# Counting the length classes with a matmul, and a new order of the first batch's preparation, in a ragged self-attention kernel

## The chip, the cores and the metric

One core of one Trainium2 chip runs the kernel. The metric is the device time of one execution in microseconds. The engines of the core are TensorE (PE; PEld is its weight load), VectorE (DVE), ScalarE (ACT), GpSimd (POOL) and SyncE (SP, which here issues most transfers). They run side by side, each with its own instruction stream, and wait for one another by semaphores.

## The reference

There are 32 sequences with up to 512 rows of 512 values, and a length for each, drawn from 64 to 511. For each sequence, only its first `seq_len` rows count, with 8 heads of 64:

```
qkv = x[b, :seq_len] @ w_qkv                      # 512 -> 3 * 512
scores = (q @ k.T) / sqrt(64)                     # per head
attn = exp(scores - max); attn = attn / (sum(attn) + 1e-08)
output[b, :seq_len] = (attn @ v) of all heads     # the rest of the rows is zero
```

## The kernel before, in words

The kernel sorts the 32 sequences by length, longest first, and works them off in pairs. Each pair belongs to a **class**: the number of rows that its longer sequence is rounded up to. `CLASSES` holds 16 values, 512, 480, 448 and so on down to 64 in steps of 32, and 340 between them. Every engine has one loop body for each class, and the index of a pair's class, read from the tile `cls`, says which body is next. Within a body, the attention of one sequence (scores, exponentials, product with v, division) is interleaved with the projections (q, k, v) of the next one.

The order on each engine is written out by hand: a `Prog` holds a list of operations for PE, ACT and DVE, and what is added first is issued first. `acquire` (L283) makes PE wait until a PSUM bank has been emptied, `evacuate` (L301) lets DVE or ACT empty it. An engine never overtakes in its own list. Everything the change touches lies in the first 25 us, before the loops.

**Sorting** (the DVE block at the end, from L1872, and the PE block). DVE makes a key of each length, finds the largest (`top`, from which SP learns the address of the longest sequence and issues the loads of its four tiles of 128 rows, `load_tiles` L1474), and ranks the keys into `onehot`. Two small matmuls (L1860) put the sorted lengths and the sorted indices into PSUM bank `pav`; DVE copies the indices to `idx` and the lengths to `n_s`. Each step goes through a `Chain` (L124), which waits for its last instruction before it issues the next one. The constants of this part (`pos_f`, `rk_f`, `sel` and others) are iotas on POOL, and the last of them raises `s_iota`, on which DVE's first step waits; the thresholds `thr_f` are three of these iotas, one row of 16 pairs by 15 classes. Then POOL makes the identity for the transposes.

**Zero matmuls.** `warm(e, n)` (L961) issues n matmuls of zeros, 512 columns each. There are nine at the start, eight behind the sorting matmuls, and six behind the first two transposes.

**The first batch** (`make_prologue`, L965). The four tiles of x land one after another. DVE casts each to half precision (`cast_x`, L1021), PE transposes it in four pieces (`transposes`, L969), and DVE or ACT copies the result to `xT` (`copy`, L981: tiles 1 and 3 on DVE, 0 and 2 on ACT). ACT meanwhile casts the weights as they land (`cast_w`, `cast_v`). The projections of the first two pairs of heads are done in halves of 256 columns, so that tiles 0 and 1 suffice to begin: `first_half(0)` to `first_half(3)`, each four matmuls, into banks a0, a1, v0 and v1, then `second_half(0)` to `second_half(3)`, each followed by DVE's cast of the whole bank to `qkT` (L1014).

PE's order is: transposes of tiles 0 and 1, six zero matmuls, transposes of tile 2; then, once banks a0 and a1 are free (copies 0 and 1) and the weights are there, first halves 0 and 1, transposes of tile 3, first halves 2 and 3; then, after copies 2 and 3, the second halves. DVE's order is: `first_masks`, casts of tiles 0, 1 and 2, copy 1, cast of tile 3, copy 3, `class_table`, then the casts of the four banks.

**The masks and the classes.** `first_masks` (L1160) clamps the lengths to at least 1 (`n_k`) and compares the row numbers with the first length, once for the keys and once for the queries; the result is needed when DVE empties the first v projection and when POOL writes a column of ones. `class_table` (L1139) compares each pair's length with the 15 thresholds, sums, converts to integers and raises `s_cls`, on which `begin_loops` (L1189) of each engine waits.

**The rest of the prologue** is a list of steps (the loop over tokens "Q2 K2 S0 S1 Q3 K3 V0 S2 S3 V1 X2 V2 X3 V3" in `make_prologue`). Q and K are projections of the next pairs of heads (DVE empties them, L423), S are scores of the first pair (ACT takes the exponential), V are projections of v (DVE empties them with the mask), X are transposes of the second batch. Banks a0 and a1 take turns, so a step waits until the bank of the step before the last has been emptied: Q2 waits for the cast of `second_half(0)`, Q3 for that of Q2, V0 for that of Q3. POOL fills some tiles (L1787), casts the second batch's first two tiles when they land (L1796) and writes the ones.

Of the kernel before, what the change touches and what calls it, by code (L numbers as in the profile page):

```python
# [7 lines left out]
FP32 = mybir.dt.float32  # L8
F16 = mybir.dt.float16
I32 = mybir.dt.int32  # L10
AF = mybir.ActivationFunctionType
ALU = mybir.AluOpType

P = 128
# [3 lines left out]
NR = 40  # L18
EARLY = 2
STEP = 32  # L20
# [10 lines left out]
DENSE_ROWS = 340  # L31
CLASSES = sorted([STEP * k for k in range(2, 17)] + [DENSE_ROWS], reverse=True)
# [120 lines left out]
def kernel(  # L153
# [17 lines left out]
    def sb(name, shape, dt):  # L171
        return nc.alloc_sbuf_tensor(name, shape, dt).ap()

    def sem(name):
        return tc.alloc_semaphore(name)
# [23 lines left out]
    pos_f = sb("pos_f", [B, B], FP32)  # L199
    pos_c = sb("pos_c", [B, 1], FP32)  # L200
    rk_f = sb("rk_f", [B, NR], FP32)
    thr_f = sb("thr_f", [1, B // 2, len(CLASSES) - 1], FP32)
    ident_f = sb("ident_f", [P, P], FP32)
    ident = sb("ident", [P, P], F16)
    cls_f = sb("cls_f", [1, B // 2], FP32)
    cls = sb("cls", [1, B // 2 + 2], I32)
    idx = sb("idx", [1, NR], I32)
    steps = sb("steps", [1, B, 4], I32)
# [25 lines left out]
    s_iota = sem("s_iota")  # L234
    s_hot = sem("s_hot")
    s_srt = sem("s_srt")
    s_id = sem("s_id")
    s_cross = sem("s_cross")
    s_cls = sem("s_cls")
# [721 lines left out]
    def warm(e, n):  # L961
        for _ in range(n):
            e.matmul(psc[:, 1, 0, :], zt16[:, 0:P], zt16[:, 0:MAXS], start=True, stop=True)

    def make_prologue():  # L965
# [6 lines left out]
        def transposes(t):  # L972
            def tr(e):
                e.wait_ge(s_c0[t], 1)
                for c in range(NC):
                    ins = e.transpose(
                        home[t][:, c * P : (c + 1) * P], x16[0][:, t, c * P : (c + 1) * P], ident
                    )
                ins.then_inc(s_t0[t], 1)

            pr.add("pe", tr)  # L981

        def copy(t, g):
            src = home[t][:, 0:D].rearrange("p (c n) -> p c n", n=P)
            dst = xT[0][:, :, t * P : (t + 1) * P]
            pr.take(g, s_t0[t])
            fn = lambda e: (e.copy if g == "act" else e.tensor_copy)(out=dst, in_=src)
            pr.add(g, lambda e: fn(e).then_inc(free[copied[t]], 1))
            pr.busy[copied[t]] = True
# [8 lines left out]
        def first_half(k):  # L998
            mms = list(part(k, 0))
            pr.add("pe", lambda e: [fn(e) for fn in mms])  # L1000
# [20 lines left out]
        def cast_x(t):  # L1021
            def fn(e):
                e.wait_ge(s_x0[t], 16)
                e.tensor_copy(out=x16[0][:, t, :], in_=x_nat[0][:, t, :]).then_inc(s_c0[t], 1)

            pr.add("dve", fn)
# [12 lines left out]
        pr.add("pe", lambda e: e.wait_ge(s_id, 1))  # L1039
        for t in range(2):  # L1040
            transposes(t)
        pr.add("pe", lambda e: warm(e, 6))
        transposes(2)
        pr.add("dve", first_masks)
        cast_x(0)
        cast_x(1)
        cast_x(2)
        copy(1, "dve")
        cast_x(3)
        copy(3, "dve")  # L1050
        pr.add("dve", class_table)
        for c in range(NC):
            cast_w(0, c, last=c == NC - 1)
        copy(0, "act")
# [5 lines left out]
        pr.add("pe", lambda e: e.wait_ge(s_wr["qk"], 1))  # L1060
        first_half(0)
        first_half(1)
        transposes(3)
        first_half(2)
        first_half(3)
        acquire(pr, "s0")
        acquire(pr, "x0")
# [41 lines left out]
        for tok in "Q2 K2 S0 S1 Q3 K3 V0 S2 S3 V1 X2 V2 X3 V3".split():  # L1109
            f, i = tok[0], int(tok[1])  # L1110
            if f == "S":
                scores(pr, i % 2, 0, 0, i, 4, MAXS)
                continue
            if f == "X":
                second_batch(i, ("act", "dve")[i % 2])
                continue
            if f == "V":
                if i == 0:
                    pr.add("pe", lambda e: e.wait_ge(s_wr["v"], 1))
                if i == 3:  # L1120
                    pr.signals += [free[b] for b in halves_av]
                vproj(pr, bank, 0, i, 4)
            else:
                if i == 2:
                    pr.add("pe", lambda e, n=2 + "QK".index(f): e.wait_ge(s_wr["qk"], n))
                qk(pr, f"a{bank}", 0, [(i, "QK".index(f))], MAXS, MAXS)
            if tok == "Q2":
                pr.add("act", cast_v)
            elif tok == "Q3":
                pr.add("pe", lambda e: begin_loops(e))  # L1130
                cast_second(2)
            elif tok == "K3":
                cast_second(3)
            bank ^= 1
        pr.add("dve", mask_table)
        pr.take("pe", s_on[0])
        return pr

    def class_table(e):  # L1139
        q = Chain(e, s_self)  # L1140
        q.tensor_tensor(
            out=thr_f,
            in0=n_s[0:1, 0:B:2].unsqueeze(2).broadcast_to([1, B // 2, len(CLASSES) - 1]),
            in1=thr_f, op=ALU.is_le,
        )
        q.reduce_sum(out=cls_f, in_=thr_f, axis=mybir.AxisListType.X)
        q.tensor_copy(out=cls[:, 0 : B // 2], in_=cls_f)
        q.memset(cls[:, B // 2 : B // 2 + 2], len(CLASSES))
        q.signal(s_cls)

    def mask(q, o, n):
        k = n.shape[1]
# [34 lines left out]
        e.reg_load(k, cls[0:1, bass.ds(e.snap(r, min_val=0, max_val=B // 2 + 1), 1)])  # L1187

    def begin_loops(e):  # L1189
        e.wait_ge(s_cls, 1)  # L1190
        r, k = e.alloc_register("pair"), e.alloc_register("cls")
        e.reg_mov(r, 0)
        e.reg_load(k, cls[0:1, 0:1])
        regs[e.engine] = (r, k)
        if e.engine == nc.tensor.engine:
            regs["next"] = e.alloc_register("next")
            e.reg_add(r, r, 1)
            e.reg_load(regs["next"], cls[0:1, 1:2])
# [209 lines left out]
    with nc.Block() as block:  # L1408
# [335 lines left out]
        def _(e):  # L1744
# [9 lines left out]
            iota(rk_f[:, B:NR], [[0, NR - B]], B - 1, 0)  # L1754
            iota(sel[:, 1, :], [[0, P]], 0, 1)
            iota(row_f, [[P, NT]], 0, 1)
            at = CLASSES.index(DENSE_ROWS)
            for a, b in ((1, at), (at, at + 1), (at + 1, len(CLASSES))):
                iota(thr_f[:, :, a - 1 : b - 1], [[0, B // 2], [-STEP, b - a]], CLASSES[a], 0,
                     b == len(CLASSES))  # L1760
            q = Chain(e, s_pself)
            q.memset(ident_f, 0.0)
            q.affine_select(
                out=ident_f, in_=ident_f, compare_op=ALU.not_equal, fill=1.0,
# [31 lines left out]
                e.tensor_copy(out=x16[1][:, t, :], in_=x_nat[1][:, t, :]).then_inc(s_xc[1], 1)  # L1796
            e.wait_ge(s_tab, 1)
            ones(0, NT, masks[:, B, :, :])
            e.wait_ge(s_cls, 1)
            e.tensor_copy(out=steps[:, :, 0], in_=idx[:, 5 : B + 5]).then_inc(s_steps, 1)  # L1800
            e.tensor_copy(
                out=steps[:, :, 1].rearrange("o (p two) -> o p two", two=2),
# [51 lines left out]
        @block.tensor  # L1854
        def _(e):
            e.wait_ge(s_zero, 1)
            warm(e, 9)
            e.wait_ge(s_hot, 1)
            for k in range(2):
                ins = e.matmul(  # L1860
                    pav[:, k * NR : (k + 1) * NR], sel[:, k, :], onehot,
                    start=True, stop=True,
                )
            ins.then_inc(full[("av", "dve")], 1)
            warm(e, 8)
            regs["far"] = e.alloc_register("far")
            prologue.run("pe", e)
            e.wait_ge(s_ini, 7)
            graph(e, "pe", None, lambda e: bridge.run("pe", e))

        @block.vector
        def _(e):  # L1872
            q = Chain(e, s_self)
            e.memset(zt, 0.0).then_inc(s_zero, 1)
            e.wait_ge(s_iota, 1)
            e.wait_ge(s_len, 16)
            e.scalar_tensor_tensor(
                out=key_r, in0=len_b.rearrange("p (b two) -> p b two", two=2)[:, :, 0],
                scalar=float(B), in1=pos_f, op0=ALU.mult, op1=ALU.add,
            ).then_inc(s_self, 1)  # L1880
            e.wait_ge(s_self, 1)
            e.nop().then_inc(s_self, -1)
            q.max(out=top_f, in_=key_r[0:1, :])
            q.tensor_copy(out=top, in_=top_f)
            q.signal(s_top)
            e.wait_ge(s_lenc, 16)
            q.tensor_copy(out=sel[:, 0, :], in_=len_c[:, 0:1].broadcast_to([B, P]))
            q.tensor_scalar(out=key_c, in0=len_c[:, 0:1], scalar1=float(B),
                            scalar2=pos_c, op0=ALU.mult, op1=ALU.add)
            q.tensor_scalar(out=cmp, in0=key_r, scalar1=key_c, scalar2=0.0,  # L1890
                            op0=ALU.is_gt, op1=ALU.add, accum_out=rank)
            q.tensor_scalar(out=onehot, in0=rk_f, scalar1=rank, scalar2=None,
                            op0=ALU.is_equal)
            q.signal(s_hot)
            e.wait_ge(full[("av", "dve")], 1)
            e.nop().then_inc(full[("av", "dve")], -1)
            q.tensor_copy(out=idx, in_=pav[0:1, NR : 2 * NR])
            q.signal(s_srt)
            q.tensor_copy(out=n_s, in_=pav[:, 0:NR])
            q.join()  # L1900
            rank_reg[0] = e.alloc_register("rank")
            e.reg_mov(rank_reg[0], 0)
            now[0] = masks[:, B, :, :]
            prologue.run("dve", e)
            begin_loops(e)
            graph(e, "dve")
# [35 lines left out]
```

## Time and profile before

| what | value |
|---|---|
| median of three runs | 335.57 us (334.88 to 336.11) |
| profiled execution | 335.28 us |
| its span, first to last instruction | 333.5 us |
| mean granted clock of PE | 0.994 |
| busy: PE, ACT, DVE, POOL | 319.4, 246.4, 204.3, 67.5 us |
| casts of tiles 0 to 3 start (DVE) | 8.17, 8.64, 10.05, 10.92 us |
| Q2 starts (PE) | 15.46 us |
| first exponential starts (ACT) | 17.71 us |

The profile is of one execution; its times count from the first instruction. The span leaves out what lies around it, here 1.8 us. A row of the timeline gives the start, the time from there to the end of the group, engine, line, operation, the tile written and those read, the shapes, the count, and in brackets how long the engine was idle before and what ended it. Waits that the sequencer of an engine ends are marked with a q (DVEq L134 is a hand-over within a `Chain`).

### The profile page before, as it was taken

Reading aid. Unit: us, or ns where it says so; the run is one execution under the profiler, and the core shown is the slowest. Engines: PE = TensorE matmul, PEld = TensorE weight load, DVE = VectorE, ACT = ScalarE, POOL = GpSimd, SP = SyncE. Lnnn points to the kernel's source line nnn. Section 1 sums busy time; section 2 is a strip of 40 time slices with the busy share of each in tenths; the row PEclk is TensorE's granted clock in tenths of the full one; section 3 lists DMA queues with packets and bytes.
Section 4 is the critical chain, followed back from the end, with each engine's and each line's share of the span. In section 5 each row is a group of like instructions: output and inputs, shape, how many; then the busy total and the mean of one; then the engine's idle time right before and its main releaser. Section 6 shows DMA issues by size and latency. Waiting matters only on the chain. (4 is left out here: it accounts for less than half of the span.)

```text
span 333.5 us, 12290 instructions
## 1 busy us (share of the span) xinstructions
PE 319.4 (96%) x4345; PEld 206.8 (62%) x4346; DVE 204.3 (61%) x578; ACT 246.4 (74%) x359; POOL 67.5 (20%) x126
## 2 busy tenths in 40 slices
PE   6899999999999999999999999999999999999990
PEld 2665545455655656656566667677777777777760
DVE  3676576546484575576566567655755566666761
ACT  4568888788979879778878887887677676766540
POOL 3634020201101211210220222022111132131331
PEclk9999999999999999999999999999999999999997
DMA  6966699766555986985886798999689767788742
GB/s 196 355 185 223 200 395 239 273 153 216 141 206 128 336 254 161 303 291 161 264 304 174 226 303 202 263 260 231 196 148 205 198 183 165 161 199 159 205 140 71
DMA packets 83249, 72.34 MB, mean 217 GB/s; under 512 B 41628, under 2 KB 64156, under 8 KB 83172
## 3 DMA queue, kind: packets, MB, share of 16 engines
q1 hardware_dynamic: 71300, 59.84, 65.9%
q10 hardware_dynamic: 11872, 11.54, 10.1%
q8 instruction: 40, 0.66, 0.9%
q14 instruction: 37, 0.30, 0.3%
HBM read 25.32 MB, written 36.70 MB: 186 GB/s over the span
## 5 line engine op out<-in xcount | busy, mean ns | idle before, releaser
L350 ACT ACTIVATE ep<-psc 128x704 f16<-128x704 f32 (+8 forms) x196 | 156.7, 848 | 43.4 <-PE psc L307 32.4
L307 PE MATMUL pa<-xT,w_r 128*128 128x224 f16 (+19 forms) x952 | 121.7, 278 | 2.0 <-DVE qkT L1014 0.7
L307 PEld LDWEIGHTS pa<-xT,w_r 128*128 128x128 f16 (+1 forms) x952 | 70.8, 97 | 29.8 <-issue 9.2
L307 PE MATMUL psc<-qkT 64*128 64x352 f16 (+17 forms) x692 | 68.0, 288 | 0.7 <-PEq L61 0.2
L423 DVE CAST qkT<-pa 128x512 f16<-128x512 f32 (+9 forms) x60 | 34.5, 577 | 44.7 <-PE pa L307 40.4
L307 PE MATMUL pa<-w_r,xT 128*128 128x512 f16 (+4 forms) x332 | 57.9, 330 | 0.0
L307 PE MATMUL pav<-v_aug,ep 128*128 128x65 f16 x1254 | 55.0, 194 | 1.2 <-PEq L61 1.2
L307 PEld LDWEIGHTS pav<-v_aug,ep 128*128 128x128 f16 x1254 | 49.0, 98 | 9.9 <-issue 2.5
L307 PE MATMUL pav<-xT,w_r 64*128 64x352 f16 (+12 forms) x392 | 50.8, 307 | 0.0
L391 ACT ACTIVATE ep<-psc 128x960 f16<-128x960 f32 (+3 forms) x48 | 42.9, 953 | 9.1 <-PE psc L307 6.0
L422 ACT CAST qkT<-pa 128x320 f16<-128x320 f32 (+8 forms) x73 | 34.1, 471 | 18.3 <-PE pa L307 14.0
L1780 POOL MEMSET v_aug<- 128x256 f16 x24 | 7.5, 313 | 186.1 <-POOLq L1368 186.1
L644 DVE SCALAR_TENSOR_TENSOR onat<-pav,masks,rcp 128x128 f32<-128x128 f32 (+1 forms) x120 | 41.4, 384 | 4.2 <-DVE rcp L621 1.6
L307 PEld LDWEIGHTS psc<-qkT 64*128 64x128 f16 x692 | 26.4, 94 | 27.8 <-issue 17.2
L1774 POOL CAST x<-x_nat 128x1536 f16<-128x1536 f32 (+3 forms) x33 | 42.0, 1272 | 7.8 <-POOLq L1368 7.6
L446 DVE TENSOR_TENSOR v_aug<-pa,masks 128x512 f16<-128x512 f32 (+1 forms) x46 | 30.7, 673 | 16.7 <-PE pa L307 16.4
L307 PEld LDWEIGHTS pav<-xT,w_r 64*128 64x128 f16 (+1 forms) x392 | 26.6, 94 | 12.3 <-issue 1.3
L307 PEld LDWEIGHTS pa<-w_r,xT 128*128 128x128 f16 (+2 forms) x332 | 22.7, 98 | 16.6 <-issue 4.1
L307 PE MATMUL pav<-w_r,xT 128*128 128x512 f16 (+3 forms) x124 | 26.9, 350 | 0.0
L307 PEld LDWEIGHTS pa<-v_aug,ep 128*128 128x128 f16 x538 | 19.6, 98 | 7.2 <-issue 3.0
L621 DVE RECIPROCAL rcp<-pav 128x8 f32<-128x8 f32 (+2 forms) x65 | 12.7, 196 | 17.5 <-PE pav L307 14.5
L307 PE MATMUL pa<-v_aug,ep 128*128 128x65 f16 x538 | 22.3, 194 | 0.0
(86 smaller groups left out, 172.3 us busy)
## 6 DMA issues: line engine op xcount, KB each, us to landing
out_dram<-zt SPq DMA_DIRECT2D x16, 768.0 KB, 5.6
x_nat<-in_x_dram SPq DMA_DIRECT2D x12, 512.0 KB
x_nat<-in_x_dram SPq DMA_DIRECT2D x5, 1024.0 KB
out_dram<-onat ACTq DMA_DIRECT2D x12, 384.0 KB, 5.4
out_dram<-onat SPq DMA_DIRECT2D x12, 384.0 KB, 4.7
x_nat<-in_x_dram SPq DMA_DIRECT2D x17, 256.0 KB, 5.6
out_dram<-onat ACTq DMA_DIRECT2D x15, 256.0 KB, 3.6
x_nat<-in_x_dram SPq DMA_DIRECT2D x4, 768.0 KB
```

Source lines behind the costliest of these rows:

```text
L307: return lambda e: e.matmul(o, lhsT, rhs, start=start, stop=stop)
L350: return e.activation(out=dst[at], in_=src[at], func=AF.Exp, scale=scale)
L391: lambda e, par=par, b=b: e.activation(out=ep[:, i, par, 0:T, 0:N], in_=psc_f[:, par, 0 : T * N].rearrange("p (t n) -> p t n", n=N), func= ...
L422: return lambda e: e.copy(out=dst, in_=src)
L423: return lambda e: e.tensor_copy(out=dst, in_=src)
L446: return lambda e: e.tensor_tensor(out=v_aug[h][:, t, lo // HD : lo // HD + n, 0:HD], in0=area[b][:, 0:w].rearrange("p (a d) -> p a d", d=HD),
L621: pr.add("dve", lambda e: e.reciprocal(out=rv, in_=den).then_inc(s_r, 1))
L644: ins = e.scalar_tensor_tensor(scalar=now[0][:, 1, t : t + 1], op0=ALU.mult, op1=ALU.mult, **ops)
L1774: e.tensor_copy(out=x16[h][:, 0:T, :], in_=x_nat[h][:, 0:T, :]).then_inc(s_xc[h], 1)
L1780: e.memset(v_aug[h][:, T - 1, NPAIR:NH, 0:HD], 0.0)
```

## The change

Four things change, all in the preparation.

1. **Classes by a matmul.** The thresholds become a column, one class a partition (`thr_c`: an iota with a step of -32 from 480, and a select that puts 340 in the last place, since the order among thresholds doesn't matter for a count). DVE compares the sorted lengths, which lie in PSUM on all partitions, with that column (`le`, 15 x 32), PE sums over the partitions by a matmul with a column of ones into bank a1, and DVE copies every second count to `cls`. `class_table` is gone. The two entries behind the last pair are set at the very start.
2. **First masks later.** `first_masks` moves on DVE from ahead of the first cast to behind the cast that empties K2.
3. **Zero matmuls.** The eight behind the sorting matmuls are split into two and six around the counting matmul; the six behind the first transposes become three.
4. **Order of the first batch.** On DVE, copy 1 goes ahead of the cast of tile 2. On PE, the transposes of tile 2 go behind first half 1, those of tile 3 behind first half 2.

Also, `idx` is copied without a hand-over on either side.

```diff
@@ make_prologue @@
         for t in range(2):
             transposes(t)
-        pr.add("pe", lambda e: warm(e, 6))
-        transposes(2)
-        pr.add("dve", first_masks)
+        pr.add("pe", lambda e: warm(e, 3))
         cast_x(0)
         cast_x(1)
+        copy(1, "dve")
         cast_x(2)
-        copy(1, "dve")
         cast_x(3)
         copy(3, "dve")
-        pr.add("dve", class_table)
...
         first_half(0)
         first_half(1)
+        transposes(2)
+        first_half(2)
         transposes(3)
-        first_half(2)
         first_half(3)
...
             if tok == "Q2":
                 pr.add("act", cast_v)
+            elif tok == "K2":
+                pr.add("dve", first_masks)
@@ begin_loops, and GpSimd's wait ahead of its copies to steps @@
-        e.wait_ge(s_cls, 1)
+        e.wait_ge(s_cls, 2)
@@ GpSimd @@
-            at = CLASSES.index(DENSE_ROWS)
-            for a, b in ((1, at), (at, at + 1), (at + 1, len(CLASSES))):
-                iota(thr_f[:, :, a - 1 : b - 1], [[0, B // 2], [-STEP, b - a]], CLASSES[a], 0,
-                     b == len(CLASSES))
             q = Chain(e, s_pself)
+            q.iota(thr_c, pattern=[[0, 1]], base=CLASSES[1], channel_multiplier=-STEP,
+                   allow_small_or_imprecise_dtypes=True)
+            q.affine_select(
+                out=thr_c, in_=thr_c, compare_op=ALU.not_equal, fill=float(DENSE_ROWS),
+                base=-(len(CLASSES) - 2), pattern=[[0, 1]], channel_multiplier=1,
+            )
+            q.memset(ones_c, 1.0)
+            q.signal(s_iota)
             q.memset(ident_f, 0.0)
@@ TensorE @@
-            warm(e, 8)
+            warm(e, 2)
+            e.wait_ge(s_le, 1)
+            k = len(CLASSES) - 1
+            e.matmul(pa[0:1, 1, 0:B], ones_c[0:k], le[0:k], start=True, stop=True).then_inc(
+                s_cnt, 1
+            )
+            warm(e, 6)
@@ VectorE @@
             e.memset(zt, 0.0).then_inc(s_zero, 1)
+            e.memset(cls[:, B // 2 : B // 2 + 2], len(CLASSES)).then_inc(s_cls, 1)
...
-            q.tensor_copy(out=idx, in_=pav[0:1, NR : 2 * NR])
-            q.signal(s_srt)
+            k = len(CLASSES) - 1
+            e.tensor_scalar(out=le[0:k], in0=pav[0:k, 0:B], scalar1=thr_c[0:k], scalar2=None,
+                            op0=ALU.is_le).then_inc(s_le, 1)
+            e.tensor_copy(out=idx, in_=pav[0:1, NR : 2 * NR]).then_inc(s_srt, 1)
             q.tensor_copy(out=n_s, in_=pav[:, 0:NR])
             q.join()
+            e.wait_ge(s_cnt, 1)
+            e.tensor_copy(out=cls[:, 0 : B // 2], in_=pa[0:1, 1, 0:B:2]).then_inc(s_cls, 1)
```

More of the change, by code (lines that the diff above doesn't have):

```diff
@@ L201 @@
     rk_f = sb("rk_f", [B, NR], FP32)
-    thr_f = sb("thr_f", [1, B // 2, len(CLASSES) - 1], FP32)
+    thr_c = sb("thr_c", [P, 1], FP32)
+    ones_c = sb("ones_c", [P, 1], F16)
+    le = sb("le", [P, B], F16)
     ident_f = sb("ident_f", [P, P], FP32)
     ident = sb("ident", [P, P], F16)
-    cls_f = sb("cls_f", [1, B // 2], FP32)
     cls = sb("cls", [1, B // 2 + 2], I32)
@@ L236 @@
     s_srt = sem("s_srt")
+    s_le = sem("s_le")
+    s_cnt = sem("s_cnt")
     s_id = sem("s_id")
@@ L1137, in make_prologue @@
         return pr
[L1139 to L1149, printed above, removed]
     def mask(q, o, n):
@@ L1798, in _ @@
             ones(0, NT, masks[:, B, :, :])
-            e.wait_ge(s_cls, 1)
+            e.wait_ge(s_cls, 2)
             e.tensor_copy(out=steps[:, :, 0], in_=idx[:, 5 : B + 5]).then_inc(s_steps, 1)
```

## The prediction

> **What bounds the kernel now.** I read the page's table of busy time first, then the timeline of the first 25 us engine by engine, because every edit lies there.
>
> ```profile
> PE 319.4 (96%) x4345; PEld 206.8 (62%) x4346; DVE 204.3 (61%) x578; ACT 246.4 (74%) x359; POOL 67.5 (20%) x126
> ```
>
> PE is busy for 96% of the span, so whatever brings PE's stream forward by a microsecond after the prologue ought to bring the end forward by as much. Hence the question: when does PE start the work that it then does without a pause? The timeline of PE answers it (start, length, line, tile, count; in brackets idle time and what ended it):
>
> ```profile
> 1.70 3.72 PE L963 MATMUL psc<-zt 128*128 128x512 f16 x9 [1.70 <-DVE zt L1874]
> ...
> 6.05 1.90 PE L963 MATMUL psc<-zt 128*128 128x512 f16 x8
> 8.75 0.78 PE L976 MATMUL psc<-ident,x 128*128 128x128 f16 x8 [0.79 <-DVE x L1024]
> 9.36 1.46 PE L963 MATMUL psc<-zt 128*128 128x512 f16 x6
> 10.66 0.39 PE L976 MATMUL psc<-ident,x 128*128 128x128 f16 x4
> 10.91 1.03 PE L307 MATMUL pa<-xT,w_r 128*128 128x256 f16 x8
> 11.78 0.39 PE L976 MATMUL psc<-ident,x 128*128 128x128 f16 x4
> 12.01 1.04 PE L307 MATMUL pav<-xT,w_r 128*128 128x256 f16 x8
> 12.88 1.04 PE L307 MATMUL pa<-xT,w_r 128*128 128x256 f16 x8
> 13.75 1.04 PE L307 MATMUL pav<-xT,w_r 128*128 128x256 f16 x8
> 15.46 1.89 PE L307 MATMUL pa<-xT,w_r 128*128 128x512 f16 x8 [0.68 <-DVE qkT L1014]
> 17.28 0.60 PE L307 MATMUL psc<-qkT 64*128 64x512 f16 x4
> 17.82 2.09 PE L307 MATMUL pa<-xT,w_r 128*128 128x512 f16 x8
> 19.75 1.06 PE L307 MATMUL pa<-w_r,xT 128*128 128x128 f16 x16
> ```
>
> The one large hole is before 15.46 (Q2): PE had finished the second halves and waited for DVE to empty bank a0. From Q2 on each row begins where the last one ends. The timeline of DVE shows why it was late:
>
> ```profile
> 7.13 0.18 DVE L142 TENSOR_SCALAR n_k<-n_s 128x40 f32<-128x40 f32 x1 [0.24 <-DVEq L134]
> 7.46 0.47 DVE L142 TENSOR_TENSOR masks<-row_f,n_k 128x4 f32<-128x4 f32 x2
> 8.17 0.90 DVE L1024 CAST x<-x_nat 128x512 f16<-128x512 f32 x2 [0.24 <-DVEq L134]
> 10.05 0.43 DVE L1024 CAST x<-x_nat 128x512 f16<-128x512 f32 x1 [0.98 <-DMA x_nat<-in_x_dram]
> 10.39 0.42 DVE L987 COPY xT<-psc 128x512 f16<-128x512 f16 x1
> 10.92 0.43 DVE L1024 CAST x<-x_nat 128x512 f16<-128x512 f32 x1
> 12.32 0.42 DVE L987 COPY xT<-psc 128x512 f16<-128x512 f16 x1 [0.97 <-DVEq L61]
> 12.66 0.39 DVE L142 TENSOR_TENSOR thr_f<-n_s,thr_f 1x240 f32<-1x240 f32 x1
> 13.19 0.39 DVE L142 TENSOR_REDUCE cls_f<-thr_f 1x16 f32<-1x240 f32 x1
> 13.73 0.43 DVE L142 CAST cls<-cls_f 1x16 int32<-1x16 f32 x1
> 14.33 0.06 DVE L142 MEMSET cls<- 1x2 int32 x1 [0.17 <-DVEq L134]
> 14.62 1.29 DVE L1014 CAST qkT<-pa 128x512 f16<-128x512 f32 x2 [0.24 <-DVEq L134]
> 15.83 1.28 DVE L1014 CAST qkT<-pav 128x512 f16<-128x512 f32 x2
> 17.02 1.28 DVE L423 CAST qkT<-pa 128x512 f16<-128x512 f32 x2
> 18.89 0.69 DVE L423 CAST qkT<-pa 128x512 f16<-128x512 f32 x1 [0.59 <-PE pa L307]
> ```
>
> The class table holds DVE from 12.66 until the next cast at 14.62, though the first second half (four of the matmuls from 12.88) was done by 13.48.
>
> **The change, part by part.**
>
> *The thresholds on POOL.* Three iotas go; an iota, a select, a memset and two hand-overs come, ahead of the signal that DVE's first operation needs.
>
> ```profile
> 1.78 0.94 POOL L1746 IOTA thr_f<- 1x80 f32 x3
> ```
> ```profile
> 3.12 0.29 POOL L142 TENSOR_SCALAR_AFFINE_SELECT ident_f<-ident_f 128x128 f32<-128x128 f32 x1 [0.25 <-POOLq L134]
> ```
> ```profile
> 3.14 0.31 DVE L1877 SCALAR_TENSOR_TENSOR key_r<-len_b,pos_f 32x32 f32<-32x32 int32 x1 [1.49 <-DMA len_b<-in_lengths_dram]
> ```
>
> A 128x128 select took 0.29 after a hand-over of 0.25; for 128x1 that is the upper bound. An estimate from these rows: 1.78, iota at most 0.31 (a third of 0.94), hand-over 0.25, select 0.29, hand-over 0.25, memset and signal some 0.2 come to 3.08 at most, about 2.9 if the one-column operations are shorter. DVE waits until 3.14 for the lengths in any case. Taken at 0, at most 0.1.
>
> *Classes by a matmul.* On DVE a compare, the index copy and n_s follow one another, then the counts are copied out. With 0.18 (the n_k row) each and some 0.4 for PE's turn, DVE is done near 7.1. On PE two zero matmuls stand ahead of the wait for the compare and six behind it; what queues behind that wait is the transposes, whose data come after 8.4. Cost 0, hidden by the landing of x. The first masks no longer stand ahead of the casts, so the first cast may start when its tile lands. The second tile:
>
> ```profile
> 5.77 0.36 SPq L1481 DMA_DIRECT2D x_nat<-in_x_dram  x1
> ```
> ```profile
> DMA to landing us min/median/max: 2.8/2.8/2.8
> ```
>
> It lands at 8.6, and its cast started at 8.64 already (second of the pair from 8.17). So moving the masks wins about 0.2 for tile 0 and nothing for tile 1.
>
> *Order of transposes.* Transposes of tile 1 end at 9.5 as before. Copy 1 is now next on DVE: 9.67 to 10.10 instead of 10.39 to 10.81, since it no longer stands behind the cast that waits until 10.05. Three zero matmuls end by 10.0. With 0.15 from a copy on DVE to PE (a0's cast ends 15.32, Q2 starts 15.46) the first halves 0 and 1 start at 10.25, not 10.91: 0.66 ahead. Then 8 matmuls of 0.109 (0.87 from 12.88 to 13.75) to 11.12, transposes 2 in 0.22 to 11.34, half 2 in 0.44 to 11.78. There transposes 3 start: the same 11.78 as before. Copy 3 stays at 12.32 to 12.74, half 3 ends at 12.44, and PE waits for copy 3 until 12.89, against 12.88. The whole 0.66 is given back, because tile 3 lands just ahead of its cast at 10.92 and now has two blocks ahead of it on PE. Three fewer zero matmuls (0.65) likewise only become a wait.
>
> *Class table gone.* The second halves end at 14.63 as before, but DVE starts its cast of a0 at 13.62 (13.48 and 0.14) and gives it free at 14.31. Q2 starts at 14.63: **0.83 ahead**. K2 at 15.49 needs the weights of the second cast here:
>
> ```profile
> 13.93 1.04 ACT L1033 CAST w_r<-w_f 128x1024 f16<-128x1024 f32 x1 [0.45 <-DMA w_f<-in_w_qkv_dram]
> ```
> ```profile
> 16.65 1.04 ACT L1077 CAST w_r<-w_f 128x1024 f16<-128x1024 f32 x1 [0.32 <-DMA w_f<-in_w_qkv_dram]
> ```
>
> It ends at 14.97, in time. The second row bounds ACT: it waits for a landing and ends at 17.69, so the exponentials start at 17.71 as now, and V0 can't start before 17.7. The scores go to 16.45, Q3 to 16.99, K3 to 18.06; K3's stream ends at 18.92, and V0 could start there instead of at 19.75.
>
> *First masks behind K2's cast.* DVE's casts run 0.60 apart: 13.62, 14.22, 14.82, 15.42, 16.02, then K2's at 16.65 (its matmuls end at 16.51) to 17.33. The masks start at 17.25, and Q3's cast, which V0 needs (it empties the bank), waits behind them. Undisturbed they take 1.04 (7.13 to 8.17): Q3's cast at 18.29 to 18.98, V0 at 19.13, 0.62 ahead. But they are no longer alone:
>
> ```profile
> 17.34 1.29 POOL L1796 CAST x<-x_nat 128x512 f16<-128x512 f32 x2 [0.50 <-DMA x_nat<-in_x_dram]
> ```
> ```profile
> 13.19 0.95 POOL L1787 MEMSET ep<- 128x1024 f32 x1
> ```
>
> The second row is the memset beside which DVE's CAST of 16 class counts took 0.43, where n_k's 40 columns took 0.18. That cast ended at 14.16, the memset at 14.14: it looks held until POOL had finished. The compare of 240 columns at 12.66 was not: 0.39 for 240 columns is what the reduction of 240 took. So a POOL instruction holds some operations of DVE on SBUF to its own end, and others not at all. A mask operation is a TENSOR_TENSOR as the free one, but its neighbour is a CAST that reads as well as writes. The bounds are 0 and the end of each POOL cast. I take the held end: two inputs beside a reading neighbour are likelier to want what it holds than one input beside a writer that did. Then n_k runs at 17.25 to 17.43, the first mask ends with POOL's first cast at 17.97, the second starts 0.15 later into the second cast (18.02 to 18.63) and ends at 18.65; with the 0.24 of the 8.17 row Q3's cast starts at 18.89. That is exactly where it starts now. V0 is at 19.75 again, and **all 0.83 is gone**.
>
> The Trainium skill speaks on this, in "SBUF — State Buffer", section "SBUF: two separate sides": GpSimd and VectorE share one pair of SBUF ports under an exclusive lock, taken by a VectorE operation in a two-port mode, or by one with two SBUF inputs only against a GpSimd operation that reads SBUF. By that rule the masks are held; the memset rows agree with both halves of it, and no row here shows a two-input operation beside a reading POOL. Without it, the two rows alone would leave it nearly even.
>
> *The sum.* Against the profiled execution (335.28, of which 333.5 are span): 0 from thresholds, count and transposes, -0.83 at Q2, +0.83 at the masks: 335.3. The median of the three runs is 0.3 higher, so the same sum reads 335.6 there; I keep 335.3, which also lies half way to the free case on that scale.
>
> **The rivals.**
>
> *Free masks.* The two-input operations run beside POOL's casts as the compare did beside the memset. V0 starts 0.62 ahead, the following S2 needs the exponential that ends at 18.7 (in time), and PE keeps it: 334.66. For it speaks the compare's row.
>
> *Slower: PE's clock falls.* The first nine zero matmuls took 0.41 each, the eight from 6.05 on 0.24 each: PE starts slow and becomes fast after some 3.3 us of work. Three zero matmuls are taken away between 10.0 and 10.7. If that let PE fall back, the decisive point is 10.25: the first halves with two sets of transposes (2.19 us of PE) would take up to twice as long, second halves would start at 14.6 and Q2 at 16.3, 0.9 late; the masks then follow K2's cast at about 19.1 and add 0.2 more: about 336.4. Against it: the hole from 7.95 to 8.75 in the profile did not slow the matmuls behind it, and the new one is shorter.
> The Trainium skill ("TensorE: Matmul & The Clock Gate", Part 1) puts the fall after an idle window of about 3.4 us, and says that transposes do not count as activity; no such hole arises here.
>
> *It doesn't reach its aim at Q2.* If copy 3 or the landing of tile 3 slips by 0.3, Q2 slips by as much, but the masks then slip too, out of POOL's way: 335.3 again. It is inside the forecast.
>
> **How the numbers follow.** Held masks 0.50 (335.3, its own range 334.9 to 335.8); free masks 0.33 (334.66); clock 0.07 (336.4, and beyond 337 if it lasts a second stretch); 0.10 for transfers that meet otherwise in the loops, to both sides. The three runs shown differ by 1.2, which blurs each case. The range from 334.0 to 336.5 takes in the free case less that blur and the clock's one stretch. About 0.5%, 1.7 us, is what a measurement of this kernel can tell from no change: no case but the clock's second stretch and the unlucky or lucky meetings goes so far. Faster 0.04, same 0.89, slower 0.07.
>
> **What would show it.** In the profile after: Q2's row near 14.6 without the bracket; the first halves near 10.25 and transposes 3 still near 11.8; the two mask rows near 17.6 and 18.1, the longer of them 0.3 to 0.6 instead of 0.16 and ending with POOL's cast rows (held), or both 0.16 (free); Q3's cast near 18.9 (held) or 18.3 (free); V0 near 19.75 or 19.1. I would be wrong if key_r moved past 3.2 (everything later by that), if zero matmuls after 6 us took 0.4, or if PE showed new waits in the loops.

## The result, and the profile after

The changed kernel's median is 334.81 us (22 runs), that of the kernel before 335.63 us (22 runs); the ratio is 0.9972, with a 95% interval of 0.9958 to 0.9985. That is 0.8 us faster, within the 0.5% that was called "same". Two later measurements of the same pair, with 12 runs of the changed kernel each, gave 0.9975 (0.9941 to 1.0008) and 1.002 (0.9983 to 1.0058). So the gain is small; only the first interval excludes 1, and the third measurement did not show it. The forecast (335.3, no change) lies inside its range, but the measured time is nearer to its second case, that of free masks (334.66). A ratio goes by all runs of both kernels that weren't slowed as a whole, and not by the medians, so the two can differ by some tenths of a per cent.

The profiled execution took 334.82 us with a span of 333.0. PE is as busy as before (first table of the page):

```profile
PE 319.8 (96%) x4343; PEld 206.3 (62%) x4344; DVE 203.9 (61%) x577; ACT 246.1 (74%) x359; POOL 67.2 (20%) x126
```

The timeline of PE, first 26 us (columns as before):

```profile
5.99 0.92 PE L966 MATMUL psc<-zt 128*128 128x512 f16 x2
...
6.94 1.47 PE L966 MATMUL psc<-zt 128*128 128x512 f16 x6
...
9.96 1.03 PE L310 MATMUL pa<-xT,w_r 128*128 128x256 f16 x8
...
11.49 0.39 PE L979 MATMUL psc<-ident,x 128*128 128x128 f16 x4
...
12.55 1.03 PE L310 MATMUL pa<-xT,w_r 128*128 128x256 f16 x8 [0.24 <-issue]
13.42 1.04 PE L310 MATMUL pav<-xT,w_r 128*128 128x256 f16 x8
14.61 1.04 PE L310 MATMUL pa<-xT,w_r 128*128 128x512 f16 x4 [0.16 <-ACT w_r L1036]
16.05 1.04 PE L310 MATMUL pa<-xT,w_r 128*128 128x512 f16 x4 [0.40 <-ACT w_r L1036]
17.02 0.61 PE L310 MATMUL psc<-qkT 64*128 64x512 f16 x4
17.56 1.90 PE L310 MATMUL pa<-xT,w_r 128*128 128x512 f16 x8
20.06 1.05 PE L310 MATMUL pa<-w_r,xT 128*128 128x128 f16 x16 [0.60 <-DVE qkT L426]
```

Q2 starts at 14.61, as forecast (14.63), but its bracket has another name: it no longer waits for DVE but for ACT's cast of weights. K2, which used to follow Q2 without a gap, waits for the next of these casts. V0 has a bracket that it did not have before: DVE empties its bank late. The timelines of ACT and DVE show both causes:

```profile
13.51 1.04 ACT L1036 CAST w_r<-w_f 128x1024 f16<-128x1024 f32 x1 [1.59 <-DMA w_f<-in_w_qkv_dram]
14.95 1.04 ACT L1036 CAST w_r<-w_f 128x1024 f16<-128x1024 f32 x1 [0.40 <-DMA w_f<-in_w_qkv_dram]
```
```profile
8.40 0.43 DVE L1027 CAST x<-x_nat 128x512 f16<-128x512 f32 x1 [0.31 <-DMA x_nat<-in_x_dram]
9.43 0.43 DVE L990 COPY xT<-psc 128x512 f16<-128x512 f16 x1 [0.60 <-DVEq L61]
...
13.19 1.29 DVE L1017 CAST qkT<-pa 128x512 f16<-128x512 f32 x2 [0.74 <-PE pa L310]
14.39 1.28 DVE L1017 CAST qkT<-pav 128x512 f16<-128x512 f32 x2
15.69 0.69 DVE L426 CAST qkT<-pa 128x512 f16<-128x512 f32 x1
17.13 0.69 DVE L426 CAST qkT<-pa 128x512 f16<-128x512 f32 x1 [0.75 <-PE pa L310]
17.74 0.17 DVE L142 TENSOR_SCALAR n_k<-n_s 128x40 f32<-128x40 f32 x1
18.06 0.93 DVE L142 TENSOR_TENSOR masks<-row_f,n_k 128x4 f32<-128x4 f32 x2
19.23 0.69 DVE L426 CAST qkT<-pa 128x512 f16<-128x512 f32 x1 [0.24 <-DVEq L134]
```

The weights landed 1.0 us later in this execution than in the one profiled before (second cast at 14.95; 13.93 before). And the two masks together took 0.93 where they took 0.47 before. POOL's row says why:

```profile
18.36 1.25 POOL L1791 CAST x<-x_nat 128x512 f16<-128x512 f32 x2 [1.61 <-DMA x_nat<-in_x_dram]
```

The first mask slipped in ahead of POOL's first cast; the second met it and ended with it, near 18.99. So one mask was held, not two. The first profiles alone would even mislead: V0 starts at 20.06, later than before (19.75), because this execution's weights were late and a mask was held. Single profiles of this kernel can only be compared from a landing onward.

### The profile page after: what moved, and what is told of

It is laid out like the page before. It is cut to its first block, busy times and chain, and to the rows that moved or that the text cites. A ratio compares the mean times of both kernels' runs of the same rounds, so it can differ in the third digit from the quotient of the medians.

```text
span 333.0 us, 12283 instructions
## 1 busy us (share of the span) xinstructions
PE 319.8 (96%) x4343; PEld 206.3 (62%) x4344; DVE 203.9 (61%) x577; ACT 246.1 (74%) x359; POOL 67.2 (20%) x126
```

## The experiments

Three questions: does an earlier start of V0 carry to the end; which part brings it; and is it POOL that holds DVE's masks? Times are medians, each beside that of the kernel before measured along with it. "C3" is the start of tile 3's cast.

**Late PE.** Eight zero matmuls more, in the kernel before:

```diff
             if f == "S":
+                if i == 0:
+                    pr.add("pe", lambda e: warm(e, 8))
                 scores(pr, i % 2, 0, 0, i, 4, MAXS)
```


> The kernel before with eight more zero matmuls on PE between K2 and S0 (1.73 us of PE at 0.216 each). Theory 'stream': from there on PE never waits for anything that does not itself come later with PE, so the end moves by all of it: +1.5 to +1.8 us, ratio 1.0045 to 1.0055. Rival 'slack': transfers and the other engines set the pace of the loops, and a late PE catches up: less than +0.8 us, ratio under 1.0025.

336.96 us against 335.56, ratio 1.004 (1.0016 to 1.0064): 1.4 us later, just below what "stream" gave and well above "slack", though the interval reaches from 0.5 to 2.1 us. In its profile (PE):

```profile
17.25 1.89 PE L963 MATMUL psc<-zt 128*128 128x512 f16 x8
19.07 0.61 PE L307 MATMUL psc<-qkT 64*128 64x512 f16 x4
```

S0 is at 19.07 instead of 17.28. What PE loses here is for the most part lost at the end.

**Table only.** The class count by matmul alone; the masks, the order and the six zero matmuls behind the first transposes are those of before. (The diff is against the changed kernel.)

```diff
-        pr.add("pe", lambda e: warm(e, 3))
+        pr.add("pe", lambda e: warm(e, 6))
+        transposes(2)
+        pr.add("dve", first_masks)
         cast_x(0)
         cast_x(1)
-        copy(1, "dve")
         cast_x(2)
+        copy(1, "dve")
...
-        transposes(2)
-        first_half(2)
         transposes(3)
+        first_half(2)
         first_half(3)
...
-            elif tok == "K2":
-                pr.add("dve", first_masks)
```


> The kernel before with only the class count by matmul (thresholds on partitions, zero matmuls split two and six); first masks, order of the transposes and the six zero matmuls as before. Theory 'stream': DVE is free after copy 3, Q2 starts 0.6 to 0.9 us ahead (if the weights have landed), no mask stands in the way, V0 is 0.6 to 0.85 ahead, end 334.7 to 335.0, ratio 0.9972 to 0.9982. Rival 'order': what the changed kernel gained came from the order and the masks: ratio 0.9995 to 1.0005.

335.08 against 335.56, ratio 0.9978 (0.9949 to 1.0008): the expected size, but not clear of none. In its profile Q2 starts at 15.35 with no bracket, right behind the second halves, though tile 3's cast came only at 11.45: C3 + 3.90, where the kernel before has C3 + 4.54. That is 0.64 ahead and not 0.83; here tile 2 landed late too (its cast started at 10.77), and so the second halves began at C3 + 2.15 instead of 1.96. PE:

```profile
13.60 1.04 PE L310 MATMUL pa<-xT,w_r 128*128 128x256 f16 x8
14.48 1.04 PE L310 MATMUL pav<-xT,w_r 128*128 128x256 f16 x8
15.35 1.89 PE L310 MATMUL pa<-xT,w_r 128*128 128x512 f16 x8
```

**Order only.** The new order and three zero matmuls in the kernel before, with its class table and early masks:

```diff
-        pr.add("pe", lambda e: warm(e, 6))
-        transposes(2)
+        pr.add("pe", lambda e: warm(e, 3))
...
+        copy(1, "dve")
         cast_x(2)
-        copy(1, "dve")
...
-        transposes(3)
+        transposes(2)
         first_half(2)
+        transposes(3)
         first_half(3)
```


> The kernel before with only the order of the first batch's transposes and copies of the changed kernel and three zero matmuls for six. The prediction's step: first halves 0.66 ahead, transposes of tile 3 and second halves as before, so nothing: second halves at C3 + 1.9 to 2.0, Q2 at C3 + 4.5. Rival: the second halves start 0.2 ahead (C3 + 1.7), copy 3 and the class table with them, and Q2 at C3 + 4.3: ratio 0.999 to 1.0.

335.44 against 335.72, ratio 0.999 (0.9959 to 1.0022): nothing that can be told. Its PE rows:

```profile
12.91 1.03 PE L307 MATMUL pa<-xT,w_r 128*128 128x256 f16 x8 [0.24 <-issue]
13.78 1.04 PE L307 MATMUL pav<-xT,w_r 128*128 128x256 f16 x8
15.76 1.46 PE L307 MATMUL pa<-xT,w_r 128*128 128x512 f16 x6 [0.94 <-ACT w_r L1033]
```

(The view ends within the last row, so it counts six of Q2's and K2's eight matmuls.) Tile 3's cast started at 11.21. So the second halves come at C3 + 1.70 instead of 1.96 (the rival), but Q2 at C3 + 4.55 as before (the prediction): the gain of 0.26 runs into the class table on DVE. What sets the end of the table is, by the rows, POOL. DVE's last cast of it began 0.2 sooner behind tile 3, and took 0.66 instead of 0.43, up to the end of POOL's third memset (DVE, POOL):

```profile
13.79 0.66 DVE L142 CAST cls<-cls_f 1x16 int32<-1x16 f32 x1
```
```profile
13.48 0.95 POOL L1787 MEMSET ep<- 128x1024 f32 x1
```

POOL starts its memsets when DVE has cast tile 3. In all five profiles of kernels with the class table (before, `late_pe`, `order_only`, `masks_late`, `key_free`) this cast takes from 0.43 to 0.81 and ends 0.02 behind that memset, at C3 + 3.24 or 3.25, and Q2 starts at C3 + 4.54 or 4.55. So in none of the five did a table that began sooner bring Q2 forward. That the memset holds the cast is read from the ends that agree; no run moved the memset alone.

The bracket of Q2 names the wrong engine: ACT's second weight cast ended just then (14.66 and 1.04), but Q2 needs only the first, which had long ended; DVE's cast of bank a0 ended at 15.61, and 0.15 later Q2 starts.

**Masks late only.** The kernel before with `first_masks` behind K2's cast:

```diff
-        pr.add("dve", first_masks)
...
+            elif tok == "K2":
+                pr.add("dve", first_masks)
```


> The kernel before with only the move of the first masks behind K2's cast; class table, order and zero matmuls as before. Theory 'stream': the masks start near 18.2, one or two of their operations are held until POOL's second cast ends near 18.6, Q3's cast starts 0.2 to 0.5 later than before, and the end is later by the same: ratio 1.0005 to 1.0015. Rival 'masks': the later masks are what made the changed kernel faster: ratio 0.997 to 0.999.

336.47 against 335.56, ratio 1.0029 (0.999 to 1.0068): 0.9 later in the median, more than expected, though the interval includes no change. The reason is another one than expected, too. Here nothing was held (DVE, then PE):

```profile
20.31 0.47 DVE L142 TENSOR_TENSOR masks<-row_f,n_k 128x4 f32<-128x4 f32 x2
21.02 0.69 DVE L423 CAST qkT<-pa 128x512 f16<-128x512 f32 x1 [0.24 <-DVEq L134]
```
```profile
21.86 1.05 PE L307 MATMUL pa<-w_r,xT 128*128 128x128 f16 x16 [0.20 <-DVE qkT L423]
```

POOL had finished both its casts, because tile 3 landed late here (its cast at 12.67) and the masks came late with it. The masks and their hand-overs take 1.05 us of DVE (19.97 to 21.02) just ahead of the cast that V0 waits for, and that by itself is enough for a wait at V0: it starts at C3 + 9.19, where the kernel before has C3 + 8.83. So the rows show a loss of 0.36 without POOL; what the rest of the 0.9 is, they don't show.

**Masks in a gap.** The changed kernel, with the masks in DVE's idle time ahead of the class counts, and without hand-overs between them:

```diff
-            elif tok == "K2":
-                pr.add("dve", first_masks)
...
             q.tensor_copy(out=n_s, in_=pav[:, 0:NR])
+            q.tensor_scalar(out=n_k, in0=n_s, scalar1=1.0, scalar2=None, op0=ALU.max)
             q.join()
+            mask(e, masks[:, B : B + 1, 0, :], n_k[:, 0:1])
+            mask(e, masks[:, B : B + 1, 1, :], n_k[:, 0:1]).then_inc(s_tab, 1)
             e.wait_ge(s_cnt, 1)
```


> The changed kernel with the first masks neither ahead of the casts by hand-overs nor behind K2, but in DVE's idle time between n_s and the class counts. Theory 'stream': no mask operation meets a cast of POOL, Q3's cast starts when Q3 is done, V0 starts when K3's matmuls end, 0.4 to 1.1 us ahead of the changed kernel's, and the end is ahead of the changed kernel's by the same: 333.8 to 334.4 us, ratio to the kernel before 0.9945 to 0.9965. Rival 'loops': the gain of the change comes from the loops (code that lies otherwise in memory) and not from the start: the same as the changed kernel, 0.9972.

334.26 against 335.56, ratio 0.9968 (0.9933 to 1.0003). PE:

```profile
15.07 1.89 PE L310 MATMUL pa<-xT,w_r 128*128 128x512 f16 x8
16.89 0.61 PE L310 MATMUL psc<-qkT 64*128 64x512 f16 x4
17.43 1.90 PE L310 MATMUL pa<-xT,w_r 128*128 128x512 f16 x8
19.34 1.05 PE L310 MATMUL pa<-w_r,xT 128*128 128x128 f16 x16
```

No bracket is left from Q2 to V0. The time alone can't tell "stream" from "loops", whose 0.9972 lies in the interval too. A second measurement, beside the changed kernel on the same chip:

> The version with the masks in the gap, once more. Theory 'stream': nothing but the weights' landing stands between the second halves and V0, so it is ahead of the changed kernel by what the masks cost there, 0.2 to 0.7 us: ratio to the kernel before 0.995 to 0.9975, and V0's row ahead of the changed kernel's by as much when told from the end of ACT's last weight cast. Rival: the weights bind both, and the two are the same within 0.2 us.

334.58 against 335.70, ratio 0.9959 (0.9934 to 0.9985), while the changed kernel got 335.68 there. This version has the lowest medians of all that were measured more than once: 1.1 to 1.3 us ahead of the kernel before, and ahead of all three medians of the changed kernel. Its weights landed late in this profile (second cast at 15.62), and K2 waited 0.24 for them; told from that cast, V0 is 0.6 ahead of the changed kernel's, as "stream" has it.

**The changed kernel again**, twice:

> The changed kernel, once more, for a second profile. Times are told from the start of tile 3's cast on DVE (C3), since the landings differ between executions. Theory 'one mask held': with the weights landing as in the kernel before (cast of the last q and k weights ended at C3 + 4.0), Q2 starts at C3 + 3.3 to 3.5 (before: C3 + 4.54), one of the two mask operations is held to the end of POOL's first cast, V0 starts at C3 + 8.0 to 8.3 (before: C3 + 8.83): the end 0.5 to 0.8 us ahead, ratio 0.9975 to 0.9985. Rival 'both held', as predicted: V0 at C3 + 8.7 to 8.9, and what was measured came from elsewhere. The ratio alone can't tell these apart; the rows can.

335.11 against 335.72, ratio 0.9975 (0.9941 to 1.0008). Neither theory held as told: no mask was held. The first tile of POOL's casts landed at 18.04 (17.29 in the kernel before), so the second mask, at 18.08, started 0.02 ahead of POOL's first cast at 18.10, and took its 0.16. DVE, POOL and PE:

```profile
17.77 0.47 DVE L142 TENSOR_TENSOR masks<-row_f,n_k 128x4 f32<-128x4 f32 x2
```
```profile
18.10 1.26 POOL L1791 CAST x<-x_nat 128x512 f16<-128x512 f32 x2 [1.25 <-DMA x_nat<-in_x_dram]
```
```profile
19.32 1.05 PE L310 MATMUL pa<-w_r,xT 128*128 128x128 f16 x16
```

> The changed kernel a third time, beside the version with the masks in the gap. Ratio to the kernel before 0.9965 to 0.9985. In its profile K2 starts 0.1 us behind the end of ACT's second weight cast (theory 'weights bind K2'), as in its first two profiles, and not where Q2's matmuls end (rival 'PE binds K2', the prediction's sum).

335.68 against 335.70, ratio 1.002 (0.9983 to 1.0058), outside what was expected: no gain here. K2 started at 15.93, which is both 0.12 behind the weight cast (14.77 and 1.04) and right behind Q2's matmuls: this profile can't tell the two theories apart; the first two did. Here one mask was held again (DVE, POOL, PE):

```profile
17.93 0.90 DVE L142 TENSOR_TENSOR masks<-row_f,n_k 128x4 f32<-128x4 f32 x2
```
```profile
18.20 1.28 POOL L1791 CAST x<-x_nat 128x512 f16<-128x512 f32 x2 [0.53 <-DMA x_nat<-in_x_dram]
```
```profile
19.90 0.49 PE L310 MATMUL pa<-w_r,xT 128*128 128x128 f16 x6 [0.57 <-DVE qkT L426]
```

**POOL waits for the masks** in the changed kernel:

```diff
+            e.wait_ge(s_tab, 1)
             for t in range(2):
                 e.wait_ge(s_x1[t], 16)
                 e.tensor_copy(out=x16[1][:, t, :], in_=x_nat[1][:, t, :]).then_inc(s_xc[1], 1)
-            e.wait_ge(s_tab, 1)
```


> The changed kernel, but POOL waits for the first masks before it casts the second batch's first two tiles. Theory 'held': both mask operations take 0.16 us, V0 starts at C3 + 7.5 to 7.8, ahead of the changed kernel's, and the end is ahead by 0.3 to 0.6 if the later casts (by up to 0.7 us) of the second batch don't come late: ratio 0.995 to 0.9975. Rival 'not POOL': the second mask operation takes 0.6 us here too.

335.11 against 335.72, ratio 0.9965 (0.9938 to 0.9993). The profile is of its longest execution (337.59). Both masks together took 0.47 there, and V0 started at 19.54, 0.15 behind DVE's cast. That is C3 + 8.14, later than expected, since K2 waited 0.25 for the weights. The timing doesn't separate it from the changed kernel, and the rows don't settle the cause alone, since the changed kernel too has an execution without a held mask.

**The lock by itself.** In the version with the masks in the gap, POOL is given one instruction that covers both masks, a copy (`lock_read`) or a memset (`lock_write`) of the same tile:

```diff
-            q.join()
+            q.signal(s_go)
+            for j in range(2):
+                e.tensor_copy(out=scr_n[:, j, :], in_=pav[:, 0:NR])
             mask(e, masks[:, B : B + 1, 0, :], n_k[:, 0:1])
...
+            e.wait_ge(s_go, 1)
+            e.tensor_copy(out=scr, in_=zt)    # or: e.memset(scr, 0.0)
```


> The version with the masks in the gap, and POOL copies 128 x 512 zeros from one tile to a spare one, started so that both mask operations fall inside it (two copies out of PSUM on DVE stand between the signal to POOL and the masks). Theory 'held by a reader': the first mask operation ends just behind POOL's copy and takes 0.3 to 0.6 us. Rival 'free': both take 0.16.

> The same with a memset of the spare tile in place of the copy, so that POOL only writes. Theory 'held by a reader': both mask operations take 0.16 us, as the two-input compare did beside a memset in the kernel before. Rival 'held by anything': the first one ends with the memset.

With the copy (DVE, then POOL):

```profile
7.21 0.31 DVE L1911 COPY scr_n<-pav 128x40 f32<-128x40 f32 x2 [0.24 <-DVEq L134]
7.43 0.54 DVE L1145 TENSOR_TENSOR masks<-row_f,n_k 128x4 f32<-128x4 f32 x2
```
```profile
7.27 0.62 POOL L1767 COPY scr<-zt 128x512 f32<-128x512 f32 x1 [3.29 <-DVEq L149]
```

With the memset:

```profile
7.43 0.23 DVE L1145 TENSOR_TENSOR masks<-row_f,n_k 128x4 f32<-128x4 f32 x2
```
```profile
7.25 0.53 POOL L1767 MEMSET scr<- 128x512 f32 x1 [3.27 <-DVEq L149]
```

The copy holds the first mask to its own end at 7.89; the memset holds nothing, and neither do the copies out of PSUM suffer. So in these runs a two-input operation of DVE was held by a POOL instruction that reads SBUF, and not by one that only writes. (Each ran once, with 336.28 and 334.91 us, which says nothing of so little.) It does not hold for every operation: the class table's last cast, which has one input, ended with a memset of POOL in five profiles.

**The first key operation.** In the kernel before it took 0.31 us, in the changed one 0.18 (the changed kernel, DVE and POOL):

```profile
3.13 0.18 DVE L1879 SCALAR_TENSOR_TENSOR key_r<-len_b,pos_f 32x32 f32<-32x32 int32 x1 [1.49 <-DMA len_b<-in_lengths_dram]
3.22 0.29 POOL L142 TENSOR_SCALAR_AFFINE_SELECT ident_f<-ident_f 128x128 f32<-128x128 f32 x1 [0.23 <-POOLq L134]
```

POOL's select, which reads, now starts after it. In `late_pe` and `table_only`, where the lengths landed later, the operation started inside the select, took 0.22 and 0.28, and ended 0.04 behind it. To test this alone, `q.memset(ident_f, 0.0)` is done twice in the kernel before.

> The kernel before with POOL's zeroing of the identity done twice, so that its select starts some 0.25 us later and misses DVE's first key operation. Theory 'held': the key operation, which in the kernel before took 0.31 and ended just behind the select, takes 0.18, as in the changed kernel, and the loads of x are issued 0.1 ahead. Rival: it takes 0.31 here too, and the select has nothing to do with it.

DVE and POOL of that run:

```profile
3.15 0.18 DVE L1878 SCALAR_TENSOR_TENSOR key_r<-len_b,pos_f 32x32 f32<-32x32 int32 x1 [1.50 <-DMA len_b<-in_lengths_dram]
```
```profile
3.49 0.29 POOL L142 TENSOR_SCALAR_AFFINE_SELECT ident_f<-ident_f 128x128 f32<-128x128 f32 x1 [0.25 <-POOLq L134]
```

As expected: 0.13 us of the chain that issues x's loads were the same kind of hold (its one time, 335.85, says nothing of so little).

**All profiles on two scales.** Landings differ between executions, so V0 is told from the start of tile 3's cast (C3) and from the start of ACT's second weight cast; `late_pe` is left out, since its zero matmuls move V0:

| kernel | C3 | second weight cast | V0 | from C3 | from the weight cast |
|---|---|---|---|---|---|
| before | 10.92 | 13.93 | 19.75 | 8.83 | 5.82 |
| key_free | 11.58 | 14.48 | 20.41 | 8.83 | 5.93 |
| masks_late | 12.67 | 15.48 | 21.86 | 9.19 | 6.38 |
| order_only | 11.21 | 14.66 | 20.04 | 8.83 | 5.38 |
| table_only | 11.45 | 14.41 | 19.62 | 8.17 | 5.21 |
| changed, one mask held | 10.86, 11.77 | 14.95, 14.77 | 20.06, 19.90 | 9.20, 8.13 | 5.11, 5.13 |
| changed, none held | 10.93 | 14.67 | 19.32 | 8.39 | 4.65 |
| pool_waits | 11.40 | 14.88 | 19.54 | 8.14 | 4.66 |
| masks_gap, gap_again | 11.77, 12.15 | 14.68, 15.62 | 19.34, 20.14 | 7.57, 7.99 | 4.66, 4.52 |
| lock_read, lock_write | 11.67, 11.08 | 14.89, 14.18 | 19.41, 18.70 | 7.74, 7.62 | 4.52, 4.52 |

Neither scale fits every kernel. With the class table, V0 follows tile 3: the same 8.83 in `before`, `key_free` and `order_only`. The 5.38 of `order_only` is no gain, then; its weights only landed later behind tile 3. Without the table, Q2 or K2 waits for the weights in the first two profiles of the changed kernel, in `pool_waits` and in `gap_again`, and there the last column is the one to read.

In `table_only`, the changed kernel's third profile and `masks_gap` no bracket names the weights, and V0 comes 0.66, 0.70 and 1.26 us sooner behind tile 3 than before. The medians of these kernels are 0.5, 0.0 to 0.8, and 1.1 to 1.3 ahead. So the rows go with the medians; with one profile of each, they don't measure them.

What follows V0 varies as well. From V0 to the end of the span it is 313.7 us in the kernel before, and 312.9, 314.1 and 313.5 in the three profiles of the changed one. The first of these ended early although its V0 was late. So a single profile can't carry a gain of 0.8, and these show no sign that the loops themselves became faster.

## Why the prediction was right or wrong

- **What bounds the kernel, and that a gain at the start carries to the end: mostly right.** 1.73 us put in came out as 1.4 (0.5 to 2.1). In the other direction, V0 came 1.26 sooner behind tile 3 in masks_gap, and the medians of that version are 1.1 to 1.3 ahead.
- **Thresholds and counting matmul at nothing: right**, with a gain of 0.13 that was not seen. The row of 3.14 with 0.31 stood in the prediction's own fence, beside a select that ended with it (3.41, the operation at 3.45); the text called a two-input operation beside a reading POOL a thing that no row shows. It was there.
- **Class table, 0.83 at Q2: right in cause, bounded otherwise.** Q2 came at 14.61 for 14.63 forecast, but that is luck: it waited for the first weight cast (13.51 and 1.04), and not for the second halves, which were done sooner than forecast. K2 was late by 0.4 in the first profile and 0.3 in the second: the weights. The prediction found them "in time" by 0.5 us, from the execution with the earliest weights of all 14 profiled. It also read the cast of 0.43 as held by a memset, and did not ask what that means for the table: by the five profiles, its end goes with POOL, whatever came ahead of it.
- **Order of the transposes, "the whole 0.66 is given back": wrong by some 0.2 to 0.4.** The step that failed is "nothing for tile 1": with x's loads issued 0.1 sooner and the masks out of the way, its cast started at 8.40 (8.52 in the second profile), not 8.64. So copy 1 started at 9.43, not 9.67, the first halves at 9.96, not 10.25, the transposes of tile 3 at 11.49, not 11.78, and the second halves at 12.55, not 12.89. In order_only, where the masks stay ahead of the casts, PE ran nearly as forecast (10.32 and 11.85). Alone this stops at the class table (order_only); with the table gone it adds to it: where no weights bind, Q2 came at C3 + 3.30 to 3.48, for 3.71 in the forecast.
- **Masks held, "all 0.83 is gone": the mechanism right, the size too large.** The step that failed is the timing of two masks against two casts: both were to be held; two profiles show one held, the third none. From the start of Q3's matmuls to V0 it is 1.91 with the masks in the gap (17.43 to 19.34), 2.05 with none held (17.27 to 19.32), and 2.50 and 2.47 with one held. So the late masks cost 0.14 or 0.56 to 0.59, where the sum had 0.83. With this and the order's term, an estimate by the same sum is -0.5 (one held) to -1.0 (none); the weights take a part of it. That the time fell inside the range owes more to the width of the range than to this sum.
- **Clock: right that it would not fall.** The zero matmuls from 6.94 on took 0.25 each, as before. The prediction's own sign against itself, zero matmuls of 0.4 behind 6 us, was nearly there: the two from 5.99 took 0.92 together. But PE was only late in becoming fast in that execution (0.60 in the other two profiles of the changed kernel), and the first transposes came at 8.25.
- What stays open: why the three measurements of the changed kernel gave 0.0 to 0.8. Whether a mask is held hangs on hundredths: the second one and POOL's first cast start at 18.37 and 18.36 in the first profile, 18.08 and 18.10 in the second (not held), 18.24 and 18.20 in the third. The landings move by a microsecond, and the step into the loops by half of one (below). How often each occurs was not counted.

## What to carry to other kernels

Before moving an operation to an "idle" stretch of its engine, look at what stands behind it in that engine's queue, and at what POOL does there: 1 us of small operations ahead of one cast that PE waits for cost 0.1 to 0.6 us of a start-up that could gain 1.3. Put such work where its engine waits for a transfer. Before shortening a chain, see what its last step ends with: here that was another engine's memset. And when a start-up is bound by landings, take their times from several profiles, not one, and count from a landing.

## What the runs showed of the hardware that was not expected

- A held DVE operation shows as a longer row, not as idle time: the mask's row starts before POOL's instruction ends and ends with it (7.43 to 7.89 beside a copy from 7.27 to 7.89). A mask that started just ahead of POOL's cast was not held (18.08 and 18.10). The Trainium skill's page "SBUF — State Buffer", section "SBUF: two separate sides", gives the rule of the shared ports, and the copy and the memset agree with both its halves: two inputs were held by a reader, and not by a writer.
- The same loads, issued within 0.25 us of the same time, landed with a wide scatter over the 14 profiles: tile 3's cast started between 10.86 and 12.67 us, the second weight cast between 13.93 and 15.62.
- PE's zero matmuls become fast at different times in different executions: the eight from about 6.05 took 1.90 us in the kernel before and 2.62 in masks_late, whose edit leaves PE's list as it was.
- The step from the prologue into the loop on PE cost nothing in some executions and half a microsecond in others of the same program. The branch into the loop body on PE's sequencer took 0.94 us in the second profile of the changed kernel and 0.42 in the first, 0.95 in gap_again and 0.41 in masks_gap; why is not shown. The second profile has this row (PE), the first has no such bracket:

```profile
24.66 0.61 PE L310 MATMUL psc<-qkT 64*128 64x512 f16 x4 [0.52 <-issue]
```
